# One split of x per norm in the feed-forward units, with results scaled by the norm's factor

## The chip, the cores and the metric

The kernel runs on one core of a Trainium2 chip. The metric is the device time of one execution in microseconds, the median of several runs. The core has a matrix engine (TensorE, PE in the profile; its weight loads have a row of their own, PEld), a vector engine (VectorE, DVE), a scalar engine (ScalarE, ACT), GpSimd (POOL) and SyncE (SP), whose queue issues most transfers.

## The reference

Two layers over 256 tokens of width 1024. Each layer is a feed-forward block, a mixer (pooling and attention, merged by gates) and a second feed-forward block. What matters here is the block with its norm:

```python
def rms_norm(x, g):
    xf = x.astype(jnp.float32)
    y = xf * lax.rsqrt(jnp.mean(xf * xf, axis=-1, keepdims=True) + EPS)
    return (y * g.astype(jnp.float32)).astype(x.dtype)

def swiglu(h, w_gate_up, w_down):
    a, b = jnp.split(h @ w_gate_up, 2, axis=-1)
    return (jax.nn.silu(a) * b) @ w_down
...
    x = x + 0.5 * swiglu(rms_norm(x, ffn1_norm), ffn1_w_gate_up, ffn1_w_down)
...
    x = x + 0.5 * swiglu(rms_norm(x, ffn2_norm), ffn2_w_gate_up, ffn2_w_down)
```

`w_gate_up` is 1024 x 5632 and `w_down` 2816 x 1024. The norm's factor is one number per token, r; the gain g is one number per feature.

## The kernel before

**Layout and numbers.** x lies with features on the partitions: 8 chunks of 128 features by 256 tokens (`x`, inside the tile `gx`). Matrix products are made from split operands: each float32 operand is a hi part (ACT, a copy to the matrix engine's rounded type) and a lo part (DVE, operand minus hi). `split` (L160 to L162) does this for weights; `hx` holds both parts of x times gain. A product is hi x hi, hi x lo and lo x hi: `chain` (L180) issues one matmul of 128x512 with the hi weights over both parts of x, and one of 128x256 with the lo weights over the hi part. The two halves of the result lie in PSUM side by side, and `drain` (L209 to L211) adds them, ACT first and then DVE.

**Units.** Weights come in units of 1 MB (two halves of 128x1024). `unit()` takes the next one that `fetch` has loaded and split; the order is `plan`, which is written out by hand (`FEED`). A unit of the first matrix gives 128 gate and 128 up features; there are 22 per block, numbers 0 to 21. `raws` holds 4 loads, `parts` six halves of hi and six of lo, so three units. `pair` multiplies a unit by hx and drains it; `post` applies silu and the product and splits the result for the second matrix. The tiles of results before `post` come from `t512` (5 buffers).

**Forms.** In three of the four blocks (all but the first) units 12 to 15 are multiplied in Strassen's way: seven products ("forms" 1 to 7) of sums of quarter blocks in place of eight. Forms of weights are summed by the transfers themselves, on GpSimd's queue, into two rooms: "a" (`sa`, tag "gd": forms 1, 5, 6, 4) and "b" (the first 8 x 256 columns of `pre`, tag "gb": forms 3 and 7). Each form in a room adds to what lies there, after the form before it has been split. Form 2 is a plain load on SyncE's queue. Forms of x are sums of quarters of the normalised x: `s1` to `s4` in `x_forms` (L431 to L434), split at L437 and L438. The products of the forms have tokens on the partitions (`by_tokens`), are combined in the token tiles `tk` (`p1`, `p5`, `c35`; tag "tok"), pass `gated`, and are transposed back by `turned`. The order is 0, 1, 2, 3, 4, 5, "1", 6, "3", 7, "2", 8, "5", 9, "7", 10, 11, "6", 16, 17, 18, "4", 19, 20, 21.

**The norm.** During the work before a block, `prep` makes hx as the split of x times gain, without r, and sums the squares in `acc`. After unit 0, `factor_spread` (L321) gives r for all partitions. Units 0 to 3 use this hx, and `post` multiplies their results by r (L367). After unit 2's matmuls `scaled_x` (L412) writes x times gain times r into `pre`; after unit 3's, `split_again` (L418) overwrites hx with its split; after unit 4's, `x_forms` builds the forms from `pre`. Units from 4 on and all forms use the normalised x and aren't scaled. The room "b" for form 3's weights is the same part of `pre` that held the scaled x. The mixer has its own `factor`, which sums the squares by token with two small matmuls (`st`) and takes their inverse root in `rsqrt`.

**What sets the order.** The program is written as one stream; a planner sorts instructions into the engines' queues by the stream's order and by when it expects their operands, and puts in the waits. Tiles of one tag take turns in the same memory, and a tile waits until the one before it has been read. Matmuls keep the stream's order; `behind` puts one instruction behind another in the planner's order.

Of the kernel before, what the change touches and what calls it, by code (L numbers as in the profile page):

```python
# [18 lines left out]
F32 = mybir.dt.float32  # L19
# [25 lines left out]
FU = NF + NF // 2 + 24  # L45
LU = FU + NF + NF // 2
GROUP = 12
FEED = (0, 1, 2, 3, 4, 5, "1", 6, "3", 7, "2", 8, "5", 9, "7", 10, 11, "6", 16, 17, 18, "4", 19, 20, 21)
FORMS = {
    "1": ("a", False, "11"), "3": ("b", False, "22"), "2": ("c", False, "21"), "5": ("a", True, "12"),  # L50
    "7": ("b", True, "12"), "6": ("a", True, "22"), "4": ("a", True, "21"),
}


C_G1, C_GM, C_G2, C_BG, C_PS, NG = 0, 8, 16, 24, 40, 44
# [3 lines left out]
def trunk_kernel(ctx: ExitStack, tc: tile.TileContext, x_in, w_in, pw_in, qkn_in, rope_in, mask_in, band_in, out):  # L59
# [35 lines left out]

    plan = []
    for base in (0, FU, LU, LU + FU):
        plan.extend([base + n if isinstance(n, int) else (base, n) for n in FEED] if base else range(NF))
        plan.extend(range(base + NF, base + NF + NF // 2))
        if base in (0, LU):  # L100
            plan.extend(range(base + NF + NF // 2, base + FU))
# [10 lines left out]
    def fetch(last=None):  # L112

        u = next(plan)
        if isinstance(u, tuple):
            ahead.append(sum_form(*u))
            return
        raw, hi, lo = buffers()
        nc.sync.dma_start(raw, w_in[u])
        for h in range(2):  # L120
            low = split(raw[:, h * HALF:(h + 1) * HALF], hi[h], lo[h])
        if last:
            behind(low, last)
        ahead.append((hi, lo))

    def buffers():
        raw = raws.tile([P, 2 * HALF], F32, name="raw", tag="raw")
        return raw, *part_buffers()

    def part_buffers():  # L130
        return [[parts.tile([P, HALF], F32R, name=n, tag=n) for _ in range(2)] for n in ("hi", "lo")]

    sums_at = {}

    def sum_form(base, f):

        n = base + GROUP
        q = {"11": (n, 0), "12": (n + 2, 0), "21": (n, 1), "22": (n + 2, 1)}
        at, add, src = FORMS[f]
        if at == "c":  # L140
            sums_at["c"] = raws.tile([P, 2 * HALF], F32, name="raw", tag="raw")
        z = sums_at[at].rearrange("p (i c) -> p i c", i=2)
        u, kh = q[src]
        w = w_in[u:u + 2, :, kh * HALF:(kh + 1) * HALF].rearrange("u p c -> p u c")
        if add:
            nc.gpsimd.dma_start(z, w, accum_op=OP.add)
        elif at == "c":
            nc.sync.dma_start(z, w)
        else:
            nc.gpsimd.dma_start(z, w)  # L150
        hi, lo = part_buffers()
        z = z.rearrange("p i (k c) -> p i k c", c=2 * P)
        for h in range(2):
            a = z[:, :, 2 * h:2 * h + 2, :]
            hv, lv = (t[h].rearrange("p (k i c) -> p i k c", i=2, c=2 * P) for t in (hi, lo))
            act(hv, a, AF.Copy)
            tt(lv, a, hv.bitcast(F32), op=OP.subtract)  # L157
        return hi, lo

    def split(w, hi, lo):  # L160
        act(hi, w, AF.Copy)  # L161
# [150 lines left out]
    def spread(dr, st):  # L312
# [5 lines left out]
        act(r, st[:, 0, :], AF.Copy)  # L318
        return r

    def factor_spread():  # L321


        ar = small.tile([P, 2, S], F32R, name="ar", tag="dr", bufs=1)
        halves(ar, acc)
        r = small.tile([P, S], F32, name="r", tag="r", bufs=2)
        h, a = (small.tile([P, S], F32, name=n, tag="sq", bufs=2) for n in "ha")
        ss = quarter("ss")[:, 0]
        for j in range(2):
            prod(ss, one_r, ar[:, j, :], j == 0, j == 1)  # L330
        act(r, ss, AF.Abs_reciprocal_sqrt, scale=1.0 / D, bias=eps)
        nc.vector.tensor_scalar(h, ss, 1.0 / D, EPS, op0=OP.mult, op1=OP.add)
        stt(a, r, -0.5, r, op0=OP.mult, op1=OP.mult)
        tt(a, a, h, op=OP.mult)
        stt(r, a, 1.5, r, op0=OP.add, op1=OP.mult)
        return r
# [4 lines left out]
    def ffn(after, n0=0, end=False, col=None):  # L341
# [19 lines left out]

        def sums():
            r.append(factor_spread())

        def post(n, scale=True):
            ab = abs_[n]
            scaled = tt(ab, ab, bc2(r[0]), op=OP.mult) if scale else None  # L367
            sg = small.tile([P, S], F32, name="sg", tag="sg", bufs=2)
            act(sg, ab[:, 0, :], AF.Silu)  # L369
            tt(sg, sg, ab[:, 1, :], op=OP.mult)  # L370
            halves(gs[n], sg)
            return scaled
# [19 lines left out]
        else:  # L392
# [6 lines left out]
            columns(ws[1], pss[1], range(4, NK))  # L399
            drain(wide(1), pss[1])  # L400

            pre = acts.tile([P, 12 * S], F32, name="pre", tag="gb")
            sums_at["a"] = acts.tile([P, 2 * HALF], F32, name="sa", tag="gd")
            sums_at["b"] = pre[:, :NK * S]
            xs = pre[:, :NK * S].rearrange("p (k s) -> p k s", s=S)
            vt = acts.tile([P, 2, GW], F32, name="vt", tag="v")
            tk = [acts.tile([P, 2, GW], F32, name="tk", tag="tok", bufs=2) for _ in range(2)]
            p1, p5, c35 = tk[0][:, 0], tk[0][:, 1], tk[1][:, 0]
            gq = {tn: vt[:, tn // 2, tn % 2 * S:(tn % 2 + 1) * S] for tn in range(4)}
            sf = {}  # L410

            def scaled_x():  # L412

                for k in range(NK):
                    c = gain[:, l_of[0], col + k:col + k + 1]
                    stt(xs[:, k, :], x[:, k, :], c, r[0], op0=OP.mult, op1=OP.mult)  # L416

            def split_again():  # L418

                for k in range(0, NK, 2):  # L420
                    act(hx[:, k:k + 2, 0, :], xs[:, k:k + 2, :], AF.Copy)
                    tt(hx[:, k:k + 2, 1, :], xs[:, k:k + 2, :], hx[:, k:k + 2, 0, :].bitcast(F32), op=OP.subtract)  # L422

            def x_forms():

                last = drained[-1]
                a11, a21 = (xs[:, :4, t * P:(t + 1) * P] for t in range(2))
                a12, a22 = (xs[:, 4:, t * P:(t + 1) * P] for t in range(2))
                s1, s2 = (pre[:, (8 + 2 * i) * S:(10 + 2 * i) * S].rearrange("p (k s) -> p k s", s=P) for i in range(2))
                s3, s4 = (vt[:, i, :].rearrange("p (k s) -> p k s", s=P) for i in range(2))  # L430
                behind(tt(s1, a22, a21, op=OP.subtract), last)  # L431
                behind(tt(s3, a11, a21, op=OP.subtract), last)
                stt(s2, s1, -1.0, a11, op0=OP.mult, op1=OP.subtract)
                stt(s4, s2, -1.0, a12, op0=OP.mult, op1=OP.subtract)  # L434
                for n, z in (("5", s1), ("3", s4), ("6", s2), ("7", s3)):
                    sh, sl = (acts.tile([P, 4, P], F32R, name="sf", tag="gates", bufs=NK) for _ in range(2))
# [18 lines left out]
            def gated(c, t, n, sign):  # L455

                c = c.rearrange("p (i j s) -> p i j s", i=2, j=2)
                sg = small.tile([P, S], F32, name="sg", tag="sg", bufs=2)
                act(by_half(sg), c[:, :, 0, :], AF.Silu, scale=sign)
                stt(by_half(gq[2 * t + n]), c[:, :, 1, :], sign, by_half(sg), op0=OP.mult, op1=OP.mult)  # L460

            def turned(n):

                pt = quarter("pt")
                for i in range(2):
                    for t in range(2):
                        keep(nc.tensor.transpose(pt[:, i, t * P:(t + 1) * P], gq[2 * t + n][:, i * P:(i + 1) * P], ident))
                g = gt["gd"][:, 2 * n:2 * n + 2]
                act(g[:, :, 0, :], pt, AF.Copy)
                tt(g[:, :, 1, :], pt, g[:, :, 0, :].bitcast(F32), op=OP.subtract)  # L470

# [2 lines left out]
            def strassen(f):  # L474
# [7 lines left out]
                if f == "1":  # L482
                    act(p1, z, AF.Copy)
                elif f == "2":
                    gated(z, 0, 0, 1.0)
                elif f == "5":
                    act(p5, z, AF.Copy)
                    tt(c35, bank["h"], p5, op=OP.add)
                elif f == "6":
                    tt(p1, z, p1, op=OP.add)  # L490
                    tt(c35, c35, p1, op=OP.add)
                    gated(c35, 0, 1, -1.0)
                    tt(p5, p5, p1, op=OP.add)
                    gated(p5, 1, 1, -1.0)
                elif f == "7":
                    tt(p5, z, p5, op=OP.add)
                    room("gb", 16, NF - 16)
                elif f == "4":
                    tt(p1, z, p1, op=OP.add)
                    gated(p1, 1, 0, 1.0)  # L500
                    room("gd", 12, 4)

            late = []
            wait = [0, 1]
            for i, n in enumerate(FEED[2:]):
                if isinstance(n, str):
                    strassen(n)
                    if n == "4":
# [1 line left out]
                    continue  # L510
                pair(unit(), wide(n))
                fetch()
                if n == 2:
                    scaled_x()
                if n == 3:
                    split_again()
                if n == 4:
                    x_forms()
                for m in wait[:2]:
                    post(m, m < 4)  # L520
                wait = wait[2:] + [n]
                for z in late:
                    z[0] -= 1
                    if z[0] == 0:
                        turned(z[1])
            for m in wait:
                post(m, False)
        gs = [gs[n] for n in range(NF)]
        for b in range(NK * NF):
            f, k = divmod(b, NF)  # L530
# [475 lines left out]
```

## Time and profile before

| | us |
|---|---|
| median of 3 runs | 1013.97 (1013.83 to 1015.1) |
| profiled execution, its time | 1015.74 |
| profiled execution, its span | 1014.0 |
| PE busy / PEld busy | 1000.9 / 906.1 |
| DVE busy | 800.2 |
| ACT busy | 638.1 |
| transfers | 202.34 MB, mean 200 GB/s |

The span runs from the first to the last instruction of the core. A row of the timeline gives the start, the duration, engine, line, operation and tiles; in brackets the engine's idle time before it and what ended it. Line 89 is the helper that records every matmul, so matmuls are told apart by their tiles: `ps` are units (and later products), `pa`, `ph`, `pe`, `pf`, `pg` the forms. Durations of neighbouring instructions overlap; what counts in a stream is the distance from start to start.

### The profile page before, as it was taken

The page shows a single profiled execution, that of the slowest core. Times are in us where ns is not written, and L with a number is a line of the kernel's source. Part 1 is how long each engine was busy: PE and PEld are TensorE (multiplying, and loading weights), DVE is VectorE, ACT ScalarE, POOL GpSimd, SP SyncE. Part 2 cuts the span into 40 slices and gives each one's busy share as a digit, 9 for nine tenths or more (in the row PEclk, how much of TensorE's full clock was granted, in tenths as well). Part 3 has the DMA queues.
Part 4 walks back from the last instruction along what each step waited for, and adds up shares of the span by engine and source line. Part 5 has one row for each costly group of instructions (what it writes and reads, how often), then busy time and mean ns, then how long its engine had stood idle before and what let it go on. Part 6 is the DMA issues. An engine that isn't in the chain of part 4 may idle for free.

```text
span 1014.0 us, 16050 instructions
## 1 busy us (share of the span) xinstructions
PE 1000.9 (99%) x6324; PEld 906.1 (89%) x6324; DVE 800.2 (79%) x1199; ACT 638.1 (63%) x1011; POOL 35.0 (3%) x64
## 2 busy tenths in 40 slices
PE   9999999999999999999998999999999999999998
PEld 8899998898899878899987889998989998888988
DVE  6998866698888888876688887666988889888752
ACT  7866655667756766665576666555677567666541
POOL 0000000002000010000001000000020000100000
PEclk9999999999999999999999999999999999999999
DMA  8856565544537478665647966555544474786540
GB/s 298 307 204 214 202 208 191 193 166 171 193 135 253 133 199 292 207 208 206 206 169 185 305 178 220 195 206 182 186 178 170 140 264 139 204 272 223 204 157 21
DMA packets 34155, 202.34 MB, mean 200 GB/s; under 512 B 3488, under 2 KB 4768, under 8 KB 13088
## 3 DMA queue, kind: packets, MB, share of 16 engines
q1 hardware_dynamic: 29184, 182.44, 50.4%
q0 software_dynamic: 4896, 18.88, 8.6%
q8 instruction: 49, 0.80, 0.3%
q14 instruction: 26, 0.21, 0.1%
HBM read 200.26 MB, written 1.05 MB: 199 GB/s over the span
## 4 chain that ended last, share of the span: by engine, by line
PE 90%; DVE 6%; DMA 2%; ACT 1%; issue 0%; SPq 0%; ACTq 0%
PE ps L89 70%; PE pt L89 7%; PE two L89 4%; PE pe L89 2%; DMA pre<-w 2%; PE pf L89 2%; DVE lo L162 1%; PE ph L89 1%; PE pa L89 1%; DVE pre L416 1%; PE sc L89 1%; PE pg L89 1%; DVE lo L157 1%; DVE ab L211 1%; DVE ab L367 1%; DVE hx L422 1%
## 5 line engine op out<-in xcount | busy, mean ns | idle before, releaser
L162 DVE TENSOR_TENSOR lo<-raw,hi 128x1024 fp32r<-128x1024 f32 (+2 forms) x348 | 412.1, 1193 | 136.9 <-ACT hi L161 135.8
L89 PE MATMUL ps<-hx,hi 128*128 128x512 f32 x1504 | 510.7, 386 | 0.8 <-ACT hi L161 0.6
L161 ACT ACTIVATE hi<-raw 128x1024 fp32r<-128x1024 f32 (+2 forms) x348 | 354.4, 1028 | 208.9 <-PE ps L89 152.7
L89 PE MATMUL ps<-hx,lo 128*128 128x256 f32 x1504 | 413.1, 275 | 6.0 <-DVE lo L162 6.0
L89 PEld LDWEIGHTS ps<-hx,hi 128*128 128x128 f32 x1504 | 284.0, 189 | 53.1 <-DVE hx L422 1.1
L89 PEld LDWEIGHTS ps<-hx,lo 128*128 128x128 f32 x1504 | 284.5, 189 | 7.1 <-DVE lo L162 7.1
L89 PE MATMUL ps<-ga,hi 128*128 128x512 f32 (+1 forms) x264 | 87.0, 376 | 0.0
L89 PE MATMUL ps<-ga,lo 128*128 128x256 f32 x256 | 69.9, 273 | 0.0
L89 PE MATMUL ps<-gb,hi 128*128 128x512 f32 (+1 forms) x198 | 65.6, 376 | 0.0
L89 PE MATMUL pt<-hi,hx 128*128 128x512 f32 x192 | 65.1, 385 | 0.0
L89 PEld LDWEIGHTS ps<-ga,hi 128*128 128x128 f32 x264 | 49.0, 188 | 8.3
L89 PE MATMUL pt<-lo,hx 128*128 128x256 f32 x192 | 52.6, 274 | 0.0
L89 PE MATMUL ps<-gb,lo 128*128 128x256 f32 x192 | 52.5, 273 | 0.0
L211 DVE TENSOR_TENSOR ab<-ps,ab 128x512 f32<-128x512 f32 x74 | 50.9, 688 | 0.8
L89 PEld LDWEIGHTS ps<-ga,lo 128*128 128x128 f32 x256 | 48.1, 188 | 0.0
L89 PE MATMUL ps<-gd,hi 128*128 128x512 f32 (+1 forms) x132 | 44.3, 376 | 0.0
L89 PE MATMUL ps<-gc,hi 128*128 128x512 f32 (+1 forms) x132 | 44.3, 376 | 0.0
L89 PE MATMUL ps<-mk,hi 128*128 128x256 f32 x256 | 44.1, 275 | 0.0
L369 ACT ACTIVATE sg<-ab 128x256 f32<-128x256 f32 x76 | 30.7, 410 | 21.3 <-DVE ab L367 10.2
L210 ACT ACTIVATE ab<-ps 128x512 f32<-128x512 f32 x74 | 42.9, 580 | 1.5 <-PE ps L89 1.5
L89 PEld LDWEIGHTS ps<-gb,hi 128*128 128x128 f32 x198 | 36.7, 188 | 6.2
L89 PEld LDWEIGHTS pt<-hi,hx 128*128 128x128 f32 x192 | 36.0, 188 | 6.8
(221 smaller groups left out, 1453.8 us busy)
## 6 DMA issues: line engine op xcount, KB each, us to landing
raw<-w SPq DMA_DIRECT2D x167, 1024.0 KB, 4.9
sa<-w POOLq DMA_DIRECT2D x12, 1024.0 KB, 9.4
pre<-w POOLq DMA_DIRECT2D x6, 1024.0 KB, 9.1
raw<-w SPq DMA_DIRECT2D x16, 256.0 KB, 5.3
out_dram<-gx SPq DMA_DIRECT2D x8, 128.0 KB, 1.9
gx<-x SPq DMA_DIRECT2D x3, 256.0 KB, 5.4
qk<-pw SPq DMA_DIRECT2D x2, 256.0 KB, 2.5
gx<-x SPq DMA_DIRECT2D x1, 300.0 KB, 2.8
```

The lines of the kernel that those rows point to most:

```text
L89: return keep(nc.tensor.matmul(*args, **kw))
L157: tt(lv, a, hv.bitcast(F32), op=OP.subtract)
L161: act(hi, w, AF.Copy)
L162: return tt(lo, w, hi.bitcast(F32), op=OP.subtract)
L210: act(t, ps[:, :, 1, :], AF.Copy)
L211: drained.append(tt(t, ps[:, :, 0, :], t, op=OP.add))
L367: scaled = tt(ab, ab, bc2(r[0]), op=OP.mult) if scale else None
L369: act(sg, ab[:, 0, :], AF.Silu)
L416: stt(xs[:, k, :], x[:, k, :], c, r[0], op0=OP.mult, op1=OP.mult)
L422: tt(hx[:, k:k + 2, 1, :], xs[:, k:k + 2, :], hx[:, k:k + 2, 0, :].bitcast(F32), op=OP.subtract)
```

## The change

For the three blocks with forms, hx stays the split of x times gain for all units; r is applied to the results. `post` multiplies every unit's result by r. For the forms, `x_forms` now runs after unit 3 (`XF`), and makes copies of x times gain on ACT (`xg`) in the two token tiles `tk`, which hold `p1`, `p5` and `c35` later; `s1` to `s4` come from these, and forms 1, 2 and 4 use hx itself. `factor_tokens` gives r by token (and its negative), and `gated` reads it as its scale. `scaled_x` and `split_again` are gone, and the part of `pre` that is room "b" holds weights only. The order of the feed is the same list. `fetch` loads units under 4 in two halves; units 0 to 3 of the first block are loaded ahead of it by other code, so it never gets such a number. `buffers` absorbs `part_buffers`; the constant `FIRST` isn't used.

```diff
+XF = 3
...
+        n = HALF if u < 4 else 2 * HALF
+        for c in range(0, 2 * HALF, n):
+            nc.sync.dma_start(raw[:, c:c + n], w_in[u, :, c:c + n])
...
+    def factor_tokens():
+
+        st = quarter("st")[:, 0, :2]
+        for t in range(2):
+            mm(st[:, t:t + 1], lhsT=acc[:, t * P:(t + 1) * P], rhs=ones[:, :1], start=True, stop=True)
+        rt = small.tile([P, 2], F32, name="rt", tag="rt", bufs=2)
+        rsqrt(rt, st, 1.0 / D)
+        nt = small.tile([P, 2], F32, name="nt", tag="nt", bufs=1)
+        nc.vector.tensor_scalar(nt, rt, -1.0, None, op0=OP.mult)
+        return rt, nt
...
         def sums():
             r.append(factor_spread())
-
-        def post(n, scale=True):
+            if not n0:
+                r.append(factor_tokens())
+
+        def post(n):
             ab = abs_[n]
-            scaled = tt(ab, ab, bc2(r[0]), op=OP.mult) if scale else None
+            scaled = tt(ab, ab, bc2(r[0]), op=OP.mult)
...
+            sums_at["a"] = acts.tile([P, 2 * HALF], F32, name="sa", tag="gd")
             pre = acts.tile([P, 12 * S], F32, name="pre", tag="gb")
-            sums_at["a"] = acts.tile([P, 2 * HALF], F32, name="sa", tag="gd")
             sums_at["b"] = pre[:, :NK * S]
-            xs = pre[:, :NK * S].rearrange("p (k s) -> p k s", s=S)
...
+            xg = [t.rearrange("p a (b s) -> p (a b) s", s=S) for t in tk]
...
-            def scaled_x():
-
+            def x_forms():
+
+                late = drained[-1]
                 for k in range(NK):
-                    c = gain[:, l_of[0], col + k:col + k + 1]
-                    stt(xs[:, k, :], x[:, k, :], c, r[0], op0=OP.mult, op1=OP.mult)
-
-            def split_again():
-
-                for k in range(0, NK, 2):
-                    act(hx[:, k:k + 2, 0, :], xs[:, k:k + 2, :], AF.Copy)
-                    tt(hx[:, k:k + 2, 1, :], xs[:, k:k + 2, :], hx[:, k:k + 2, 0, :].bitcast(F32), op=OP.subtract)
-
-            def x_forms():
-
-                last = drained[-1]
-                a11, a21 = (xs[:, :4, t * P:(t + 1) * P] for t in range(2))
-                a12, a22 = (xs[:, 4:, t * P:(t + 1) * P] for t in range(2))
+                    behind(act(xg[k // 4][:, k % 4, :], x[:, k, :], AF.Copy, scale=gain[:, l_of[0], col + k:col + k + 1]), late)
+                (a11, a21), (a12, a22) = ([z[:, :, t * P:(t + 1) * P] for t in range(2)] for z in xg)
...
-                behind(tt(s1, a22, a21, op=OP.subtract), last)
-                behind(tt(s3, a11, a21, op=OP.subtract), last)
+                tt(s1, a22, a21, op=OP.subtract)
                 stt(s2, s1, -1.0, a11, op0=OP.mult, op1=OP.subtract)
+                tt(s3, a11, a21, op=OP.subtract)
                 stt(s4, s2, -1.0, a12, op0=OP.mult, op1=OP.subtract)
...
+                sc = r[1][sign][:, t:t + 1]
                 sg = small.tile([P, S], F32, name="sg", tag="sg", bufs=2)
-                act(by_half(sg), c[:, :, 0, :], AF.Silu, scale=sign)
-                stt(by_half(gq[2 * t + n]), c[:, :, 1, :], sign, by_half(sg), op0=OP.mult, op1=OP.mult)
+                act(by_half(sg), c[:, :, 0, :], AF.Silu, scale=sc)
+                stt(by_half(gq[2 * t + n]), c[:, :, 1, :], sc, by_half(sg), op0=OP.mult, op1=OP.mult)
...
-                if n == 2:
-                    scaled_x()
-                if n == 3:
-                    split_again()
-                if n == 4:
+                if n == XF:
                     x_forms()
                 for m in wait[:2]:
-                    post(m, m < 4)
+                    post(m)
...
             for m in wait:
-                post(m, False)
+                post(m)
```

More of the change, by code (lines that the diff above doesn't have):

```diff
@@ L47 @@
 GROUP = 12
-FEED = (0, 1, 2, 3, 4, 5, "1", 6, "3", 7, "2", 8, "5", 9, "7", 10, 11, "6", 16, 17, 18, "4", 19, 20, 21)
+XF = 3
+FIRST = 5
 FORMS = {
@@ L52, with feed_order, feed_units @@
 }
+def feed_order():
+    return [0, 1, 2, 3, 4, 5, "1", 6, "3", 7, "2", 8, "5", 9, "7", 10, 11, "6", 16, 17, 18, "4", 19, 20, 21]
+def feed_units(base):
+    return [base + n if isinstance(n, int) else (base, n) for n in feed_order()]
 C_G1, C_GM, C_G2, C_BG, C_PS, NG = 0, 8, 16, 24, 40, 44
@@ L97, in trunk_kernel @@
     for base in (0, FU, LU, LU + FU):
-        plan.extend([base + n if isinstance(n, int) else (base, n) for n in FEED] if base else range(NF))
+        plan.extend(feed_units(base) if base else range(NF))
         plan.extend(range(base + NF, base + NF + NF // 2))
@@ L118, in fetch @@
         raw, hi, lo = buffers()
-        nc.sync.dma_start(raw, w_in[u])
+        n = HALF if u < 4 else 2 * HALF
+        for c in range(0, 2 * HALF, n):
+            nc.sync.dma_start(raw[:, c:c + n], w_in[u, :, c:c + n])
         for h in range(2):
@@ L124, in fetch @@
         ahead.append((hi, lo))
[L126 to L131, printed above, removed]
     sums_at = {}
@@ L150, in sum_form @@
             nc.gpsimd.dma_start(z, w)
-        hi, lo = part_buffers()
+        _, hi, lo = buffers(False)
         z = z.rearrange("p i (k c) -> p i k c", c=2 * P)
@@ L158, in sum_form, with buffers @@
         return hi, lo
+    def buffers(raw=True):
+        raw = raws.tile([P, 2 * HALF], F32, name="raw", tag="raw") if raw else None
+        hi = [parts.tile([P, HALF], F32R, name="hi", tag="hi") for _ in range(2)]
+        lo = [parts.tile([P, HALF], F32R, name="lo", tag="lo") for _ in range(2)]
+        return raw, hi, lo
     def split(w, hi, lo):
@@ L467, in turned @@
                         keep(nc.tensor.transpose(pt[:, i, t * P:(t + 1) * P], gq[2 * t + n][:, i * P:(i + 1) * P], ident))
-                g = gt["gd"][:, 2 * n:2 * n + 2]
+                g = gt["gd"][:, 2 * n:2 + 2 * n]
                 act(g[:, :, 0, :], pt, AF.Copy)
@@ L484, in strassen @@
                 elif f == "2":
-                    gated(z, 0, 0, 1.0)
+                    gated(z, 0, 0, 0)
                 elif f == "5":
@@ L491, in strassen @@
                     tt(c35, c35, p1, op=OP.add)
-                    gated(c35, 0, 1, -1.0)
+                    gated(c35, 0, 1, 1)
                     tt(p5, p5, p1, op=OP.add)
-                    gated(p5, 1, 1, -1.0)
+                    gated(p5, 1, 1, 1)
                 elif f == "7":
@@ L499, in strassen @@
                     tt(p1, z, p1, op=OP.add)
-                    gated(p1, 1, 0, 1.0)
+                    gated(p1, 1, 0, 0)
                     room("gd", 12, 4)
@@ L504, in ffn @@
             wait = [0, 1]
-            for i, n in enumerate(FEED[2:]):
+            for i, n in enumerate(feed_order()[2:]):
                 if isinstance(n, str):
```

## The prediction

> **What bounds the kernel now.** I read the page first: its busy shares and the groups of instructions.
>
> ```profile
> PE 1000.9 (99%) x6324; PEld 906.1 (89%) x6324; DVE 800.2 (79%) x1199; ACT 638.1 (63%) x1011; POOL 35.0 (3%) x64
> ```
>
> TensorE (PE) sets the time: 1000.9 of 1014.0 us. A change can win only where PE waits or runs slowly. The windows view finds those places.
>
> ```profile
> core 0: us, PE busy (x) PEld busy (x) DVE busy (x) ACT busy (x) POOL busy (x), PEclk, DMA share, GB/s
> 345.00:360.00 15.00, 14.97 (x90) 13.19 (x89) 15.00 (x26) 11.50 (x22) 1.21 (x1) 1.00 0.28 76
> 360.00:375.00 15.00, 12.89 (x66) 10.86 (x65) 11.22 (x17) 9.00 (x14) 1.93 (x2) 0.89 0.74 209
> 375.00:441.00 66.00, 66.00 (x396) 59.15 (x395) 56.61 (x73) 45.43 (x67) 2.37 (x2) 1.00 0.79 248
> 540.00:556.00 16.00, 12.18 (x59) 10.05 (x59) 11.96 (x17) 9.83 (x16) 1.93 (x2) 0.89 0.74 197
> 865.00:880.00 15.00, 13.02 (x68) 11.26 (x67) 11.59 (x17) 9.47 (x15) 1.94 (x2) 0.89 0.78 210
> ```
>
> After the stretch and its length the columns are the busy times of PE, PE's weight loads, VectorE (DVE), ScalarE (ACT) and GpSimd, then the granted clock. Each feed-forward stage with forms (three of them; I call them norms 1, 2, 3) has one bad stretch: PE idles 2 to 4 us, the granted clock falls to 0.89, and DVE has just been busy without a gap (15.00 of 15.00). The timeline of PE gives the losses one by one. First the list of waits, for unit 4's place, then the timeline of norm 1:
>
> ```profile
> PEld ps L89 <- DVE hx L422: 1.1, 3, 0.4
> ```
>
> ```profile
> 361.35 0.39 PE L89 MATMUL ps<-hx,hi 128*128 128x512 f32 x1
> 363.74 0.38 PE L89 MATMUL ps<-hx,lo 128*128 128x256 f32 x1 [2.00 <-DVE lo L162]
> 364.30 0.54 PE L89 MATMUL ps<-hx,hi 128*128 128x512 f32 x1
> 367.83 0.28 PE L89 MATMUL ps<-hx,lo 128*128 128x256 f32 x1
> 367.95 0.39 PE L89 MATMUL ps<-hx,hi 128*128 128x512 f32 x1
> 368.18 0.28 PE L89 MATMUL ps<-hx,lo 128*128 128x256 f32 x1
> 368.30 0.38 PE L89 MATMUL ps<-hx,hi 128*128 128x512 f32 x1
> ```
>
> Undisturbed, a hi and a lo matmul take 0.35 us from start to start (367.95 to 368.30), of which the hi 0.23 and the lo 0.12. So norm 1 loses (a) at unit 4, on the renewed hx, some 0.3 (three weight loads waited 1.1 in all, and run in part beside the matmul before); (b) at unit 6, on the lo part of its weights: 2.39 - 0.23 = 2.2; (c) a slow stretch from 364.30 to 367.83: six hi and five lo in 3.53 us where they need 6 x 0.23 + 5 x 0.12 = 1.9 at most, so 1.6. Sum 4.1. Norms 2 and 3:
>
> ```profile
> 541.19 0.38 PE L89 MATMUL ps<-hx,hi 128*128 128x512 f32 x1
> 543.58 0.38 PE L89 MATMUL ps<-hx,lo 128*128 128x256 f32 x1 [2.00 <-DVE lo L162]
> 548.68 0.27 PE L89 MATMUL ps<-hx,lo 128*128 128x256 f32 x1
> 551.26 0.38 PE L89 MATMUL ph<-lo,sf 128*128 128x256 f32 x1 [0.78 <-DVE lo L157]
> 552.15 0.63 PE L89 MATMUL ph<-hi,sf 128*128 128x512 f32 x1
> 555.35 0.48 PE L89 MATMUL ps<-hx,hi 128*128 128x512 f32 x1
> 866.25 0.38 PE L89 MATMUL ps<-hx,hi 128*128 128x512 f32 x1
> 868.62 0.38 PE L89 MATMUL ps<-hx,lo 128*128 128x256 f32 x1 [1.98 <-DVE lo L162]
> ```
>
> Norm 2: (a) 0.3, (b) 2.2, (d) at form "3", first on its hi and then on its lo part, 2.58 - 0.35 = 2.2, and (c) after it, 552.15 to 555.35: five pairs in 3.20 where 1.75 do, 1.5. Sum 6.2. Norm 3: (a) 0.3, (b) 2.1, (c) 1.6 (taken as in norm 1), (d) none. Sum 4.0. **In all 14.3 us**: (a) 0.9, (b) 6.5, (c) 4.7, (d) 2.2. Two causes stand behind (b) and (d):
>
> ```profile
> 340.31 3.25 DVE L416 SCALAR_TENSOR_TENSOR pre<-gx,r 128x256 f32<-128x256 f32 x8
> 343.48 1.29 DVE L367 TENSOR_TENSOR ab<-ab,r 128x512 f32<-128x512 f32 x2
> 348.95 0.69 DVE L211 TENSOR_TENSOR ab<-ps,ab 128x512 f32<-128x512 f32 x1
> 349.56 1.29 DVE L422 TENSOR_TENSOR hx<-pre,hx 128x512 fp32r<-128x512 f32 x2
> 356.97 0.70 DVE L431 TENSOR_TENSOR pre<-pre 128x512 f32<-128x512 f32 x1
> 362.44 1.24 DVE L162 TENSOR_TENSOR lo<-raw,hi 128x1024 fp32r<-128x1024 f32 x1
> 360.38 0.74 POOL L150 DMA_DIRECT2D pre<-w  x1 [2.14 <-DVE vt L434]
> 368.77 2.01 ACT L156 ACTIVATE hi<-pre 128x1024 fp32r<-128x1024 f32 x2 [5.89 <-DMA pre<-w]
> ```
>
> Unit 6's lo came at 362.44, at the end of a DVE queue without a gap. And form "3" can load its weights only at 360.38, when the last reader of the scaled x has left `pre` (L434); ACT gets them 8.4 us later.
>
> **What the change removes.** Per norm, from DVE: the eight products of L416 (340.31 to 343.48: 3.2 us) and the four splits of L422 at 0.60 us start to start (348.95 to 349.56): 2.4. Together 5.6 us, all in front of unit 6's lo. From ACT four hi copies. With them (a) goes, since hx isn't rewritten. And `pre` holds no x any more: form "3" may load as soon as its room is free, which in norm 2 is when the stage before has read it. The transfers before it show how early that is:
>
> ```profile
> 303.14 0.91 POOL L150 DMA_DIRECT2D sa<-w  x1 [64.99 <-DVE mg L827]
> 504.30 0.74 POOL L150 DMA_DIRECT2D sa<-w  x1 [100.42 <-PE ps L89]
> ```
>
> Form "1" is issued 57 us ahead of unit 6's wait in norm 1 and 37 us ahead in norm 2. Form "3" is the next on GpSimd's queue and goes to the neighbouring room; its 8.4 us then end long before it is used. So (d) goes. The split of a load in two for units under 4 never runs: the first four units are loaded outside `fetch`.
>
> **What it adds.**
>
> ```profile
> L367 DVE TENSOR_TENSOR ab<-ab,r 128x512 f32<-128x512 f32 x34 | 23.0, 690 | 0.4
> L421 ACT ACTIVATE hx<-pre 128x512 fp32r<-128x512 f32 x12 | 7.1, 616 | 0.0
> L272 ACT ACTIVATE hx<-gx 128x256 fp32r<-128x256 f32 x48 | 23.5, 498 | 6.2 <-DVE gx L549 3.6 <-DVE gx L878 1.4 <-DMA gx<-x 1.2
> 193.79 0.34 PE st L89 x4
> 196.44 0.16 DVE L293 TENSOR_SCALAR h<-st 128x2 f32<-128x2 f32 x1 [0.35 <-ACT rt L291]
> 197.16 0.43 DVE L307 TENSOR_TENSOR dg<-ident,rt 128x256 f32<-128x256 f32 x1
> ```
>
> - PE: the two sums by token, which the mixer already makes: 0.34 us in the chain of waits (the row at 193.79) per norm, on the path. **3 x 0.34 = 1.0 us lost.** They hold one of four PSUM quarters until DVE has read it.
> - DVE: 14 more products by r (units 4 to 11 and 16 to 21), 14 x 0.60 = 8.4 us per norm; only unit 4's stands ahead of unit 6's lo. The factor by token: four small instructions in 0.72 us (196.44 to 197.16) and a fifth like them, 0.9. The other 13 products lie in the feed behind unit 6. There DVE is busy 56.6 of 66.0 us while PE has no gap (the stretch from 375); some ten of them fall into it, 6 us, which makes 95%. I cost them at nothing, because DVE's idle time there is 9.4 us; with that cover gone each costs 0.6 (a rival below).
> - ACT: eight gain-scaled copies of x (L272's shape: 0.50 us, start to start some 0.40 if they overlap as L422's do, 0.69 every 0.60) for four hi copies (L421, by the same count 0.52): +1.1 us. ACT is busy 11.5 of 15 there. The small inverse root beside the one that stands there needs no other function, so I count no table load.
> - Scales that are read from a column in `gated`: some 0.1 us each on ACT, off the path.
>
> **The new wait.** `s1` on DVE now waits for ACT's copies, which are put behind unit 3's drain (348.95 + 0.6 = 349.6). Eight of them take 3.2 (4.0 without overlap): `s1` starts at about 352.8 (353.6), not 356.97. Behind it in DVE's queue stand the form differences, the drains and unit 6's lo, for which PE waits. Old distance from `s1` to the end of that lo: 362.44 + 1.14 - 356.97 = 6.6; now also unit 4's drain and product (1.2) and perhaps one split of form "1" (1.1): 7.8 to 8.9, so 360.6 to 361.7 (362.5). PE gets there at 361.35 + 0.23 - 0.3 + 0.34 = 361.6. From the other side, by load alone: DVE's gapless queue from 340.31 loses 5.6 and gains 1.5, and the lo ends at 359.5. So (b) ends between no wait and, if both splits of form "1" and a slow planner come in front, 2 us as now. I take 0.4 us per norm, near the nearest rows, **1.2 in all**, and expect no slow stretch behind so short a gap.
>
> The sum: 14.3 - 1.0 - 1.2 = 12.1 gained. The profiled execution took 1015.74 us (span 1014.0 and 1.7 around it); the median shown is 1013.97. From the median: 1013.97 - 12.1 = **1001.9 us** (1003.6 against the profiled one).
>
> On (c) the row speaks first: a gap of 2.2 us (361.57 to 363.74) is followed by 3.5 us at half speed. The Trainium skill ("TensorE: Matmul & The Clock Gate", Part 1) states that PE's clock falls to half after an idle window of about 3.4 us and warns of gaps over 3 us; by that, our gaps would be too short, the slow stretches would have another cause and stay, and the sum would be 4.7 smaller. The trace disagrees with the length: no window without a gap shows a clock under 1.00.
>
> **Rivals.**
> 1. *DVE is still late at unit 6.* For it: the new wait sits in front of the same lo, and the bound reaches 2 us. Against: 4.1 us of load less. A wait of 1.2 with a slow stretch of 1.6 costs 3 x (0.8 + 1.6) = 7.2 more: 1009.1; the whole old loss, (b) and (c) kept, 11.2 - 1.2 = 10.0 more: 1011.9.
> 2. *The slow stretches stay though the gaps go.* 1001.9 + 4.7 = 1006.6. Against: each begins within 3 us of a gap.
> 3. *Slower: DVE becomes the bound in the feed*, units 7 to 21. For it: 95% busy, in order, and its waits are for ACT's hi parts, which wait for PE; such waits can't be used freely. If none can, ten products of 0.6 per norm fall on the path, 18 us: 1001.9 + 18 = 1019.9. It decides from about two thirds of them (12.1 of 18). Against: 9.4 us idle, and weight parts for three units, which let DVE run ahead.
> 4. *Form "3" doesn't load earlier*, because the room or GpSimd's order holds it at 360.38. PE then comes to it sooner and waits for the same 368.77: nothing but (a) is gained, against the 1.0 of the sums by token: 1014.0. Against: the room's old reader is gone.
>
> **How the numbers follow.** Forecast 0.56, rival 1 0.24, rival 2 0.07, rival 3 0.08, rival 4 0.05. Low end: no wait left and some unlisted tenths, 999. High end: most of rival 1, 1010; outside lie the end of rival 1, 3 and 4, about 0.19. Runs of this kernel lie 1.3 us apart, so about 0.2% (2 us) is what can be told from no change. Faster than 1011.9 (0.2% under the median): the forecast, rival 2 and nearly all of rival 1, 0.86; same: rival 4 and a crumb, 0.06; slower: rival 3, 0.08.
>
> **What would show it.** The group of L416 gone and the scaling group x76 instead of x34; a GpSimd load of `pre` at about 303 and 506; no PE gap at unit 4, 6 and form "3"; PEclk 1.00 in those windows. A `[.. <-DVE lo L162]` at unit 6 is rival 1; DVE at 100% in 375 to 441 with PE gaps there is rival 3; `[.. <-DMA pre<-w]` on ACT is rival 4.

## The result and the profile after

The changed kernel takes 1001.98 us (median of 4 runs, 1001.85 to 1003.7) where the kernel before takes 1014.18 beside it (1013.83 to 1015.1): a ratio of the means of 0.9882, with its 95% interval [0.9865, 0.9899]. The profiled execution took 1002.1 us with a span of 1000.3, 13.7 less than before's.

First the page of the changed kernel, its busy shares and the shares of the engines in the chain that ended last:

```profile
PE 995.0 (99%) x6336; PEld 903.1 (90%) x6336; DVE 811.2 (81%) x1220; ACT 646.3 (65%) x1026; POOL 35.1 (4%) x64
...
PE 99%; DMA 0%; DVE 0%; ACT 0%; SPq 0%; issue 0%
```

DVE is busier than before (811.2 against 800.2 us), and the kernel is faster. Of the chain 99% is PE now (90% before). The windows around the place where norm 1 had its bad stretch, and a window of the feed behind it (the columns are those of the prediction):

```profile
341.00:356.00 15.00, 15.00 (x92) 13.50 (x91) 14.02 (x25) 13.61 (x25) 1.23 (x1) 1.00 0.63 169
356.00:371.00 15.00, 15.00 (x91) 13.36 (x90) 14.86 (x22) 13.35 (x21) 1.22 (x1) 1.00 0.60 140
371.00:437.00 66.00, 66.00 (x397) 59.14 (x396) 60.45 (x80) 44.24 (x64) 2.41 (x2) 1.00 0.77 240
```

PE is busy 15.00 of 15.00 us where it had 12.89, the clock stays at 1.00, and DVE still has idle time (14.02 of 15, and 60.45 of 66 behind). The list of what PE waits for has three rows for unit 6 and form "3" in the kernel before (each with the total in us, the number of waits and the longest):

```profile
PE ps L89 <- DVE lo L162: 6.0, 3, 2.0
PE ph L89 <- ACT hi L156: 1.0, 1, 1.0
PE ph L89 <- DVE lo L157: 0.8, 1, 0.8
```

They are gone in after, and the two rows left are both at the kernel's start:

```profile
PE busy L99 <- DVE eps L260: 1.1, 1, 1.1
PE ps L99 <- ACT hi L172: 0.9, 1, 0.9
```

To add it up, take the distance in the trace from the norm's sum of squares (`ss`) to the last group of transposes of the forms (`pt`). The two ends in norm 1, for before and then for after:

```profile
334.05 0.39 PE L89 MATMUL ss<-ar,one_r 128*128 128x256 f32 x2
441.38 0.60 PE L467 MATMUL pt<-ident,vt 128*128 128x128 f32 x4
```

```profile
334.50 0.39 PE L99 MATMUL ss<-ar,one_r 128*128 128x256 f32 x2
437.65 0.60 PE L481 MATMUL pt<-ident,vt 128*128 128x128 f32 x4
```

So 107.33 us before and 103.15 after. The same reading in all three norms, and in the experiments that follow:

| kernel | norm 1 | norm 2 | norm 3 | sum | `ss` of the first block at |
|---|---|---|---|---|---|
| before | 107.33 | 109.28 | 106.95 | 323.56 | 30.4 |
| after | 103.15 | 103.15 | 103.15 | 309.45 | 30.9 |
| e1, room alone | 104.09 | 105.14 | 104.88 | 314.11 | 32.4 |
| e2, room shared | 103.15 | 103.15 | 103.14 | 309.44 | 30.2 |
| e4, load back | 106.80 | 108.24 | 107.49 | 322.53 | 32.3 |
| e8, no factor by token | 102.72 | 102.74 | 102.73 | 308.19 | 30.4 |
| e9, room shared and forms late | 108.44 | 110.25 | 108.03 | 326.72 | 32.0 |
| e10, three splits later | 107.81 | 110.77 | 110.20 | 328.78 | 32.2 |
| e11, factor from the diagonal | 102.72 | 102.74 | 102.73 | 308.19 | 30.7 |

A stage in which PE never waits takes 102.73 us without the added sums by token and 103.15 with them. Against 308.19 the kernel before lost 15.4 us; after, 1.26 (3 x 0.42, the sums by token) are left. The stages gained 14.1; the span fell 13.7, since this execution started 0.45 later. The last column is used in the section on the hardware: in four of these executions the start itself cost 1 to 2 us more, which none of the edits explains.

### The profile page after: what moved, and what is told of

The parts are those of the page before. It is cut to its first block, busy times and chain, and to the rows that moved or that the text cites. A ratio compares the mean times of both kernels' runs of the same rounds, so it can differ in the third digit from the quotient of the medians.

```text
span 1000.3 us, 16151 instructions
## 1 busy us (share of the span) xinstructions
PE 995.0 (99%) x6336; PEld 903.1 (90%) x6336; DVE 811.2 (81%) x1220; ACT 646.3 (65%) x1026; POOL 35.1 (4%) x64
## 4 chain that ended last, share of the span: by engine, by line
PE 99%; DMA 0%; DVE 0%; ACT 0%; SPq 0%; issue 0%
PE ps L99 78%; PE pt L99 7%; PE two L99 4%; PE pe L99 2%; PE pf L99 2%; PE pa L99 2%; PE sc L99 1%; PE ph L99 1%; PE pg L99 1%; PE pt L655 1%; PE y L99 1%; DMA raw<-w 0%; PE tp L611 0%; PE pt L481 0%; PE st L99 0%; PE ss L99 0%
## 5 line engine op out<-in xcount | busy, mean ns | idle before, releaser
L391 DVE TENSOR_TENSOR ab<-ab,r 128x512 f32<-128x512 f32 x76 | 52.0, 687 | 0.9
```

## The experiments

The change has three parts that could each explain the gain: DVE has 5.6 us less to do ahead of unit 6 (*relief*); form "3"'s room is free, so its weights can be loaded early (*room*); and the forms of x are built one unit earlier (*early forms*). Theory at the outset: relief ends the gap at unit 6 and, with it, the slow stretch; room ends the gap at form "3" of norm 2; the rest adds nothing. Its rivals: the room or the early forms do it without the relief.

**e1: the room alone.** The kernel before with the scaled x in the token tiles, so that `pre` holds weights only. What reads the scaled x (`split_again`, `x_forms`) reads it there; DVE's work is unchanged.

```diff
-            xs = pre[:, :NK * S].rearrange("p (k s) -> p k s", s=S)
+            xg = [t.rearrange("p a (b s) -> p (a b) s", s=S) for t in tk]
...
-                    stt(xs[:, k, :], x[:, k, :], c, r[0], op0=OP.mult, op1=OP.mult)
+                    stt(xg[k // 4][:, k % 4, :], x[:, k, :], c, r[0], op0=OP.mult, op1=OP.mult)
```

> The kernel before, with one part of the change: the scaled x lies in the token tiles, and form 3's room holds weights only; DVE's work and the second split stay. Theory (two causes, DVE's queue for the gap at unit 6 and the room for the gap at form 3): only the 2.2 us at form 3 in norm 2 and perhaps the 1.5 us slow stretch behind it go, so 1010.5 to 1012.0 us, with the 2.0 us waits for the lo part at unit 6 still there in all three norms and GpSimd's load of form 3 some 50 us earlier. Rival (the late load is the main cause, and the crowding at unit 6 comes with it): most of the gain is here, 1006 us or less.

Measured: 1006.98 us (1005.0 to 1008.49), 0.9919 [0.9892, 0.9947]; by the table 9.5 of the 15.4 us are recovered (323.56 - 314.11). The theory missed: not only form "3", the gap at unit 6 shrank as well, to two waits of at most 0.33 us in each norm, though DVE does the same instructions. Its list of waits, and then DVE's timeline in norm 1:

```profile
PE ps L89 <- DVE lo L162: 1.4, 6, 0.3
```

```profile
361.40 0.69 DVE L434 SCALAR_TENSOR_TENSOR vt<-pre,tk 128x512 f32<-128x512 f32 x1
...
362.68 1.23 DVE L162 TENSOR_TENSOR lo<-raw,hi 128x1024 fp32r<-128x1024 f32 x1
363.81 0.69 DVE L438 TENSOR_TENSOR sf<-vt,sf 128x512 fp32r<-128x512 f32 x1
364.41 0.69 DVE L211 TENSOR_TENSOR ab<-ps,ab 128x512 f32<-128x512 f32 x1
...
365.95 1.23 DVE L162 TENSOR_TENSOR lo<-raw,hi 128x1024 fp32r<-128x1024 f32 x1
```

The same stretch of the kernel before:

```profile
359.37 0.70 DVE L434 SCALAR_TENSOR_TENSOR vt<-pre 128x512 f32<-128x512 f32 x1
...
360.31 0.70 DVE L211 TENSOR_TENSOR ab<-ps,ab 128x512 f32<-128x512 f32 x1
360.91 0.70 DVE L438 TENSOR_TENSOR sf<-vt,sf 128x512 fp32r<-128x512 f32 x1
...
361.84 0.70 DVE L438 TENSOR_TENSOR sf<-pre,sf 128x512 fp32r<-128x512 f32 x1
```

From `s4` (L434) to unit 6's lo it is 1.28 us in e1 (361.40 to 362.68) and 3.07 before (359.37 to 362.44): in before, a drain (L211) and two splits of forms (L438) stand ahead of the lo, in e1 behind it. That the planner changed the order because form "3"'s weights come early is likely, but not shown. The lo thus comes 1.8 us sooner; the lo of the unit's second half (365.95) is now waited for too. To see what the two cost, take the start of each matmul, from the stage's start, against the same matmul in e8, which never waits: unit 6 costs 2.9 us over the three norms in e1 and 6.5 before. More than half of the loss at unit 6 was thus the order of the queue, not its length. With the gaps this short no slow stretch followed, in any of the three norms.

**e2: after, with the copies in form "3"'s room.** It takes the free room away and keeps relief and early forms.

```diff
-            xg = [t.rearrange("p a (b s) -> p (a b) s", s=S) for t in tk]
+            xg = [pre[:, i * 4 * S:(i + 1) * 4 * S].rearrange("p (b s) -> p b s", s=S) for i in range(2)]
```

> The kernel after, with the copies of x in form 3's room instead of the token tiles; all else is as after. Form 3's load then waits for the last form difference (356.2 us in norm 1), takes 8.4 us and is split by about 367.1; PE comes to form 3 at 367.4. Theory (DVE's load and the earlier forms decide, the room matters little once the forms are early): 1002 to 1003.5 us, waits at form 3 of 0.5 us at most per norm. Rival (the free room is needed): a wait of about 2 us at form 3 in each norm with a slow stretch, 1009 us or more.

Measured: 1001.67 (1001.47 to 1003.75), 0.9873 [0.9848, 0.9898], as after. The timelines of GpSimd, ACT and PE in norm 1, one row of each, show why:

```profile
356.14 0.74 POOL L155 DMA_DIRECT2D pre<-w  x1 [4.33 <-ACT ga L244]
```

```profile
363.27 1.06 ACT L161 ACTIVATE hi<-pre 128x1024 fp32r<-128x1024 f32 x1 [3.40 <-DMA pre<-w]
```

```profile
366.65 0.39 PE L99 MATMUL ph<-hi,sf 128*128 128x512 f32 x1
```

The load starts only at 356.14, but that is early enough: ACT has the weights 7.1 us later, and PE's first product of form "3" starts at 366.65 without a wait. With early forms the free room isn't needed.

**e3: after, with the forms built one unit later.** It takes early forms away and keeps relief and room.

```diff
-XF = 3
+XF = 4
```

> The kernel after, with the forms built after unit 4 (as before) instead of unit 3. Theory (what closes the gap at unit 6 is the 5.6 us less of DVE work; its lo part now ends 2.7 us ahead of PE): no gap opens, 1002 us within 1. Rival (the earlier place of the forms is what closes it): the forms' eight DVE instructions, 4.8 us, then run into unit 6's lo part, a wait of 1 to 2 us with a slow stretch per norm, 1009 to 1012 us.

Measured: 1001.56 (1001.02 to 1001.78), 0.9866 [0.9843, 0.9889]; no gap. With room, early forms aren't needed either. Early forms were not tried alone, without the relief.

**e9: both taken away, so that relief stands alone** (the edits of e2 and e3 together).

> The kernel after with both: the copies of x in form 3's room, and the forms built after unit 4. DVE's relief alone is left. Theory (the relief closes the gap at unit 6 but not the one at form 3; for that one either the free room or the early forms are enough, and one of them is needed): no gap at unit 6; the last form difference ends at about 360.6 us in norm 1, form 3's load lands 7 to 8.4 us later, PE waits 2.2 to 3.5 us for its hi and 0.9 for its lo part, 3.1 to 4.4 us per norm with slow stretches of 0 to 1.6: 1011 to 1020 us. Rival (DVE's relief alone carries the whole gain): 1002 us.

Measured: 1017.11 (1016.42 to 1020.48), 1.0018 [1.0005, 1.003]: relief alone gains nothing at all. PE's waits:

```profile
PE ph L99 <- ACT hi L161: 6.1, 3, 2.3
PE ph L99 <- DVE lo L162: 2.3, 3, 0.8
```

The gap at unit 6 is gone, as forecast, and PE then stands at form "3" in all three norms, 2.0 us on the hi part and 0.8 on the lo part in the mean, with slow stretches behind. In the kernel before the gap at unit 6 had hidden this late load almost wholly in norms 1 and 3.

**e10: before, with three of the four form splits put behind unit 6.** Nothing is removed; only the place of 1.8 us of DVE work in the queue changes, and of ACT's three copies that go with it. `split_forms` is the loop body that stood in `x_forms`.

```diff
-                for n, z in (("5", s1), ("3", s4), ("6", s2), ("7", s3)):
+                rest.extend((("5", s1), ("6", s2), ("7", s3)))
+                split_forms((("3", s4),))
...
+                if n == 6:
+                    split_forms(rest)
```

> The kernel before, with one change of order: the splits of the forms 5, 6 and 7 of x come after unit 6; nothing is removed. In DVE's queue two splits (1.2 us) leave the place ahead of unit 6's lo part and one product of 0.34 us takes it. Theory (the order of DVE's queue ahead of that lo part sets the gap, with the same load in all): the gap at unit 6 falls from 2.2 to about 1.3 us in each norm; 2.6 us less, and 0 to 4.7 for slow stretches: 1006.5 to 1011.5 us. Rival (the load of the stretch sets it): the gap stays 2.0 us or more, 1014 us.

Measured: 1022.61 (1015.97 to 1026.72), 1.0068 [1.0045, 1.009]: slower, where both theories said faster or the same. PE's waits:

```profile
PE ph L89 <- ACT hi L156: 6.3, 3, 2.2
PE ps L89 <- DVE lo L162: 3.1, 3, 1.1
PE ph L89 <- DVE lo L157: 2.1, 3, 0.8
```

The wait at unit 6 fell as intended, from 2.0 to 1.0 us in the mean (3.1 over three). But form "3"'s load is not tied to PE. GpSimd's and ACT's rows in norm 1:

```profile
361.93 0.74 POOL L150 DMA_DIRECT2D pre<-w  x1 [1.89 <-DVE vt L434]
```

```profile
371.08 2.00 ACT L156 ACTIVATE hi<-pre 128x1024 fp32r<-128x1024 f32 x2 [6.06 <-DMA pre<-w]
```

This execution began 1.8 us later than before's (the last column of the table); less that, the load is issued at 360.1 (360.38 before) and the hi copy starts at 369.3 (368.77 before). PE arrives some 2.5 us sooner than before in norms 1 and 3, 0.7 in norm 2, and waits there in all three norms. The two waits stand in series against one transfer that doesn't move with PE: what the first gives up the second takes. Set against e8 as above, PE leaves the waits at form "3" 5.0 to 5.2 us late here, and 4.2 to 4.9 before. The total even grew, by 5.2 us in the three stages: 1.7 are this later end, 2.7 come from slow stretches behind form "3" (4.4 us in norms 2 and 3, against 1.7 in norm 2 before), and 0.8 are small steps in the feed of norm 3.

**e4 and e5: DVE's load put back into after.** e5 adds at unit 2 eight products into a scratch tile (the size of those of L416), e4 these and four subtractions like L422's at unit 3.

```diff
+                if n == 2:
+                    dm = small.tile([P, 2, S], F32, name="dm", tag="dr", bufs=1)
+                    for k in range(8):
+                        c = gain[:, l_of[0], col + k:col + k + 1]
+                        stt(dm[:, k % 2, :], x[:, k, :], c, r[0], op0=OP.mult, op1=OP.mult)
+                if n == 3:
+                    for k in range(0, 8, 2):
+                        tt(dm, x[:, k:k + 2, :], hx[:, k:k + 2, 0, :].bitcast(F32), op=OP.subtract)
```

> The kernel after, with the removed DVE work put back as work on a scratch tile that nothing reads: eight products of 128x256 after unit 2 and four differences of 128x512 after unit 3, 5.6 us per norm. Theory (DVE's queue sets unit 6's lo part, and a gap of PE brings the slow stretch): 5.6 less 2.7 of lead and 1.2 of idle time gives a wait of about 1.7 us per norm at unit 6, with slow stretches of 1.6 behind it: about 1012 us; without slow stretches 1007. Rival (not the load, but the rewriting of hx or the room brought the gaps): 1002 us, no gap.

> The kernel after, with only the eight products of 128x256 put back as work that nothing reads, 3.2 us of DVE per norm. Theory (unit 6's lo part has 2.7 us of lead, and DVE 1.2 us of idle time ahead of it): no gap, 1002 us within 1. Rival (the lead is used up sooner, since the order in the queue and not the sum decides): a gap of 0.5 to 1 us per norm, 1003.5 to 1009 us by whether slow stretches follow.

Measured: e5 1002.1 (1001.23 to 1003.77), 0.987 [0.9848, 0.9891], no gap; e4 1016.54 (1014.47 to 1019.42), 1.0014 [0.9996, 1.0033]. PE's waits and two rows of DVE's timeline in e4:

```profile
PE pa L99 <- DVE lo L162: 8.1, 6, 2.3
```

```profile
360.11 1.23 DVE L162 TENSOR_TENSOR lo<-sa,hi 128x1024 fp32r<-128x1024 f32 x1
...
363.99 1.23 DVE L162 TENSOR_TENSOR lo<-sa,hi 128x1024 fp32r<-128x1024 f32 x1
```

The load brings the loss back, but not where it was: PE waits at form "1" (`pa`, `sa`), one step ahead of unit 6, 0.6 and then 2.4 us per norm, more than expected, and only norm 2 has a slow stretch. So after has between 3.2 and 5.6 us of DVE's time to spare here, and once that is used up, the place of the wait is the planner's choice.

**e6 and e7: the 14 added products.** e6 leaves out the scaling of the results of units 4 to 11 and 16 to 21 in the three blocks; e7 makes each of these products twice, the second into scratch.

```diff
-            scaled = tt(ab, ab, bc2(r[0]), op=OP.mult)
+            scaled = tt(ab, ab, bc2(r[0]), op=OP.mult) if n0 or n < 4 else None
```

```diff
             scaled = tt(ab, ab, bc2(r[0]), op=OP.mult)
+            if not n0 and n >= 4:
+                tt(dm[0], ab, bc2(r[0]), op=OP.mult)
```

> The kernel after without the 14 added products per norm: the results of units 4 to 11 and 16 to 21 aren't scaled by r. Theory (the products lie in DVE's idle time): the same time, 1002 us within 0.7. Rival (some of them reach the path): faster by up to 14 x 0.6 x 3 = 25 us; by a tenth of it, 2.5 us, were one in ten on the path.

> The kernel after, with each of the 14 products done a second time into a scratch tile. DVE is busy 60.4 of 66.0 us in the feed behind unit 7; ten to twelve more of 0.6 us make 66.5 to 67.7. Theory (DVE has cover up to about 5 us per norm and becomes the bound beyond it): small gaps, 1 to 3 us per norm with or without slow stretches, 1005 to 1012 us. Rival (DVE's idle time is waiting and can't be used, all new work falls on the path): 3 x 14 x 0.6 = 25 us, 1027 us. Rival (there is more cover, since PE's lead of three units hides it): 1002 us.

Measured: e6 1001.72 (1001.24 to 1001.87), 0.9862 [0.9846, 0.9878], as after. e7 1006.87 (1005.49 to 1008.04), 0.9913 [0.9894, 0.9931]. In e7 the three stages add up to 309.44 us, as in after: the feed carries 28 products without a gap. What is lost comes behind it, at the start of the second matrix. e7's waits:

```profile
PE ps L99 <- DVE gb L245: 2.9, 3, 1.0
```

DVE has fallen behind by the end of the feed, and the products of the second matrix wait 1.0 us for the last results. That explains 1.1 us per norm; another 1.2 us in all comes in steps of 0.12 in the last second matrix, and that stays unexplained.

**e8 and e11: the factor by token.** e8 leaves it out (the forms' results are not scaled by r). e11 takes it from r itself, on DVE: r times the identity, summed along the row, in place of the two matmuls and the inverse root.

```diff
-    def factor_tokens():
+    def factor_tokens(r):
...
-        st = quarter("st")[:, 0, :2]
-        for t in range(2):
-            mm(st[:, t:t + 1], lhsT=acc[:, t * P:(t + 1) * P], rhs=ones[:, :1], start=True, stop=True)
+        dg = small.tile([P, 2, P], F32, name="dg", tag="sg", bufs=2)
+        tt(dg, r.rearrange("p (a b) -> p a b", b=P), bc2(ident), op=OP.mult)
         rt = small.tile([P, 2], F32, name="rt", tag="rt", bufs=2)
-        rsqrt(rt, st, 1.0 / D)
+        nc.vector.tensor_reduce(rt, dg, axis=AX.X, op=OP.add)
```

> The kernel after without the factor by token: the forms' results aren't scaled by r, and the two sums by token with their inverse root are left out. Theory (their two matmuls stand on PE's path): 3 x 0.34 = 1.0 us faster, 1001.0 us. Rival (they fit between other matmuls): the same, 1002.0 us.

> The kernel after, with the factor by token taken from r on DVE in place of PE: r times the identity, summed along the row, which picks the diagonal; it gives the same numbers. It takes DVE one product of 128x256 and one sum of 256 for four small instructions, about the same 0.7 us, and takes the two matmuls from PE. Theory (they stand on PE's path): 3 x 0.34 = 1.0 us faster than after, 1001.0 us, no new gap. Rival (DVE's two instructions push a lo part late in the first units): 1002 us or more, with a gap at units 3 to 6.

Measured: e8 1000.32 (999.64 to 1002.52), 0.9853 [0.9833, 0.9872]; e11 1000.74 (1000.48 to 1001.95), 0.9854 [0.983, 0.9877]. The intervals overlap with after's, but the stages don't: 102.73 us in each norm of both against 103.15. So the sums by token cost 3 x 0.42 = 1.26 us, and e11 has them for nothing. It computes all that the reference does and is by its stages the fastest of the versions that do.

## Why the prediction was right

The forecast of 1001.9 us was met (1001.98), and what it named to look for is there: L391 counts x76, L416's products are gone, PE has no gap at unit 4, at unit 6 or at form "3". Form "3"'s load comes even earlier than the forecast 303 and 506, in norms 1 and 3 ahead of form "1"'s. The timeline of GpSimd in after:

```profile
286.03 0.90 POOL L155 DMA_DIRECT2D pre<-w  x1 [47.44 <-ACT pk L751]
303.59 0.73 POOL L155 DMA_DIRECT2D sa<-w  x1 [16.65 <-DVE mg L837]
...
502.56 0.73 POOL L155 DMA_DIRECT2D pre<-w  x1 [1.26 <-PE ps L99]
...
780.51 0.77 POOL L155 DMA_DIRECT2D pre<-w  x1 [47.35 <-ACT pk L751]
```

**The sum, term by term.** Against the profile the forecast was 14.3 - 1.0 - 1.2 = 12.1 us. The stages show 15.4 - 1.26 - 0 = 14.1.

- *The losses, 14.3.* They were 15.4. Set against e8, (a) 0.9 and (b) 6.5 are right, (c) is 5.2 instead of 4.7 and (d) 2.6 instead of 2.2. The list of single gaps missed smaller ones: in norm 1 the first products of form "3" start 0.50 us apart where 0.22 do. In norm 1 the working of (c) also has a slip: 6 x 0.23 + 5 x 0.12 is 1.98, not 1.9.
- *The sums by token, 1.0.* They cost 1.26: the chain shows 0.34 per norm, and the first matmuls behind them need another 0.08.
- *The wait left at unit 6, 1.2.* This was the term farthest off; there is none. DVE's timeline in after:

```profile
353.38 0.69 DVE L444 TENSOR_TENSOR pre<-tk 128x512 f32<-128x512 f32 x1 [0.53 <-ACT tk L440]
...
358.52 1.22 DVE L173 TENSOR_TENSOR lo<-raw,hi 128x1024 fp32r<-128x1024 f32 x1
359.65 0.68 DVE L451 TENSOR_TENSOR sf<-pre,sf 128x512 fp32r<-128x512 f32 x1
```

`s1` starts at 353.38, within the forecast 352.8 to 353.6. But unit 6's lo ends at 359.65, 6.3 us behind it, not 7.8 to 8.9: it was estimated from the old order with a product and a split of form "1" added, while in after `s3` and both splits of form "1" are done before `s1` starts, and a split of a form (L451 at 359.65) has gone behind the lo. The other bound, by load alone (359.5), came nearest: on the clock of before, whose stage began 0.45 us sooner, the lo ends at 359.2. The chain of waits shows PE there, in one run of units' products up to form "3":

```profile
362.09 5.35 PE ps L99 x32
```

So the lo is some 2.4 us early.

Of the median little of this is seen, since the profiled execution of before was a long one (1015.74 against 1014.18), and the surplus of 2.0 us in the stages went into that difference and the later start. The forecast took the gain from the long execution and the time from the median; two errors of opposite sign made it exact, which is luck.

**The reasons.** Products behind unit 6 at no cost: right (e6), with more cover than was claimed, since DVE is busy 60.45 of 66.0 us, 92% and not 95%, and e7's doubling brings no gap in the feed. Slow stretches go with the gaps: right in after and e1, though not every gap has one (the last section says which). The step that failed is the treatment of (b), unit 6, and (d), form "3", as separate terms with a cause each. e9 and e10 show that they stand in series: with (b) alone gone, (d) rises from 2.2 us in one norm to about 3.2 in all three (e9's waits of 6.1 and 2.3, and a tenth or two behind each), and nothing is gained. And (b) was put down to DVE's load, while e1 takes more than half of it away with the load unchanged, through the queue's order. The forecast came out since the change removes both, and it did so twice over: relief needs either the room (e3) or the early forms (e2) beside it, not both.

**The rivals.** Rival 1 (DVE late at unit 6) lies between e5 and e4: 3.2 us more of load and no wait, 5.6 more and the whole gain is lost, though at form "1". Rival 2 (slow stretches without gaps) is refuted by the clock of 1.00 in all of after's windows. Rival 3 (DVE the bound in the feed) is refuted for the feed by e7; e7's loss lies behind it, in the second matrix. Rival 4 (form "3" not loaded earlier) didn't come about, but its mechanism is real, and its time was 0.3% off: e9 is that case, at 1017.11 where 1014.0 was said.

## What to carry to other kernels

Waits that follow one another on an engine are not terms of a sum: before a gap is counted as gain, ask when the next operand would be there if PE came earlier by as much, and look first at transfers whose start does not move with PE. In a queue without idle time the position of the instruction that is waited for matters as much as the work in front of it, so bound such a wait by order and by load, and try the order by an experiment. What a gap of PE costs beyond its own length depends on how much of it falls into one window of the clock (next section), so price that as a chance. For an account to tenths of a microsecond compare the same stage between two events in the traces, not spans or medians, which carry the start and the luck of the slow stretches.

## What the hardware showed that was not expected

**The same gap is sometimes followed by a slow stretch and sometimes not.** e10 has both; PE's timeline at form "3" in norm 1 and in norm 2:

```profile
372.18 0.49 PE L89 MATMUL ph<-hi,sf 128*128 128x512 f32 x1 [2.12 <-ACT hi L156]
373.44 0.38 PE L89 MATMUL ph<-lo,sf 128*128 128x256 f32 x1 [0.77 <-DVE lo L157]
373.66 0.38 PE L89 MATMUL ph<-hi,sf 128*128 128x512 f32 x1
...
552.64 0.67 PE L89 MATMUL ph<-hi,sf 128*128 128x512 f32 x1 [2.21 <-ACT hi L156]
553.90 0.58 PE L89 MATMUL ph<-lo,sf 128*128 128x256 f32 x1 [0.59 <-DVE lo L157]
554.27 0.63 PE L89 MATMUL ph<-hi,sf 128*128 128x512 f32 x1
```

In norm 1 the products run at full speed at once (0.38), in norm 2 at about half (0.63 from 554.27 on, until 559.39). The traces show what decides it. Within one execution all changes of the granted clock lie a whole number of 3.41 us apart (in before at 364.40, 367.81, 552.13, 555.54, 869.57 and 872.98), so the clock is set for one such window at a time. e10's windows at the two places, in the columns of the prediction:

```profile
368.48:371.89 3.41, 1.58 (x10) 1.18 (x8) 0.00 (x0) 0.81 (x1) 0.00 (x0) 1.00 0.98 411
371.89:375.30 3.41, 2.34 (x12) 1.85 (x13) 3.13 (x4) 3.41 (x6) 0.47 (x1) 1.00 0.00 0
...
549.39:552.80 3.41, 1.20 (x8) 0.83 (x6) 0.18 (x1) 1.27 (x2) 0.00 (x0) 1.00 0.89 340
552.80:556.21 3.41, 2.82 (x9) 2.05 (x10) 3.41 (x4) 3.41 (x6) 0.93 (x1) 0.50 0.03 14
```

In norm 1 PE's idle time is divided over two windows (busy 1.58 and 2.34 of 3.41 us), and the clock stays. In norm 2 a window holds 2.21 us of it (busy 1.20), and the next has half the clock. In the stages of before, e4, e9 and e10 all seven windows with 1.98 us or more of idle time are followed by one at half clock, none with 1.7 or less is, and of the five from 1.81 to 1.92 two are. So the 2.0 us at unit 6 in before are punished in norms 1 and 3, but not in norm 2, where a border cuts them into 0.32 and 1.68. A slow stretch is one window long, or two where the first holds idle time of its own (0.59 us in e10 and 0.74 in e9, both in norm 2).

The Trainium skill ("TensorE: Matmul & The Clock Gate", Part 1) speaks of a free-running window of some 3.4 us. The traces agree: the borders lie differently in each execution (one is at 5.59 in after, at 6.00 in before, at 10.08 in e10). By that page it takes an idle window of that length to lose the clock; here some 2 us within one window were enough. A position that differs from run to run would also explain e10's spread, though only one of its ten runs has a trace: they reach from 1015.97 us, at a granted clock of 1.000, to 1026.72, at 0.990, and 0.010 of the clock over 1020 us is 10.2 us, what six windows at half clock lose (1.71 each).

**Full speed comes late in some starts.** The first unit's rows in after and in e10:

```profile
6.21 0.48 PE L99 MATMUL ps<-hx,hi 128*128 128x512 f32 x1 [0.94 <-ACT hi L172]
```

```profile
5.90 0.80 PE L89 MATMUL ps<-hx,hi 128*128 128x512 f32 x1 [0.64 <-ACT hi L161]
```

In e10 half speed lasts until 9.94. The trace's clock record has full speed for the first time (the view of windows prints 1.00 ahead of it too) at 5.59 in after and at 10.08 in e10. In the four executions with a late start (the last column of the table) it comes at 9.48 to 10.33, in the others by 6.97. In these four the window that holds PE's wait for the first unit has 0.64 to 0.85 us of idle time, and full speed is granted only after the next one; in the other executions the window right before the grant has 0.62 or less.

**A column as scale.** The groups of instructions show `gated`'s DVE product with the column of r by token as its scale in after, and with a constant in before:

```profile
L474 DVE SCALAR_TENSOR_TENSOR vt<-tk,nt,sg 128x256 f32<-128x256 f32 x6 | 2.6, 478 | 0.0
```

```profile
L460 DVE SCALAR_TENSOR_TENSOR vt<-tk,sg 128x256 f32<-128x256 f32 x9 | 3.8, 423 | 0.0
```

The column costs 55 ns for each. It is off the path: e8, with constants, and e11, with the column, have the same stages.
